# Padding that gives all matmul operands one offset within 512 bytes, and a write of normed rows split over two steps of the experts

## The chip, the cores and the metric

One core of a Trainium2 chip runs one program. The metric is the device time of one execution in microseconds (us), taken several times. Matmuls run on TensorE (PE; its weight loads are PEld), elementwise work on VectorE (DVE) and ScalarE (ACT), and GpSimd (POOL) issues a few of the transfers (DMA). The queue of SyncE (SP) issues the weight transfers.

## The reference

Two layers of a generator over 256 latent rows and 256 context rows of 1024 numbers. The first layer has a spatial-gating branch and an attention branch, then a dense SwiGLU of width 2816 (the FFN). The second has a gated recurrence, then a mixture of eight SwiGLU experts (the MoE), each of width 2816, of which every latent row uses two:

```python
def swiglu(t, w1, w3, w2):
    return (jax.nn.silu(t @ w1) * (t @ w3)) @ w2

logits = (t @ router_w).astype(jnp.float32)
top_v, top_i = lax.top_k(logits, TOP_K)
gk = jax.nn.softmax(top_v, axis=-1)
for e in range(N_EXPERTS):
    out = out + gates[:, e:e + 1] * swiglu(t, w1[e], w3[e], w2[e])
```

Everything is float32.

## The kernel before, in words

**Products.** A float32 product is made from three products of rounded halves (`mm3`, lines 358 to 361): both operands are cut into a high and a low part of type float32r, and PE runs high times high (line 359), high times low (360) and low times high (361). Weights come from DRAM in units of 1 MB (or 768 KB) into "raw" tiles; ACT casts half a unit to its high part `wh` (line 126) and DVE subtracts to get the low part `wl` (line 127). Raw tiles form a ring and `wh`/`wl` tiles another; a transfer waits on SP until the raw tile that it fills was cut by ACT and DVE.

**Places in SBUF.** Tiles are laid out pool after pool, each tile rounded up to 32 bytes per partition. Pools that open later begin where the ones below them end, so a small tile's size moves everything behind it. Modulo 512 bytes, summed up from the tile sizes, the start addresses of the float32r operands before are:

| operand | where | start modulo 512 before | after |
|---|---|---|---|
| `wh`, `wl` (cut weights) | all stages | 128 | 128 |
| `hH`, `hL` (cut activations), `hLa`, `hLb` | all stages | 128 | 128 |
| `mg` (cut hidden rows of an expert) | MoE, second product | 128 | 128 |
| `gH`, `gL` (cut hidden rows of the FFN) | FFN, second product | 192 | 128 |
| `xTH` (high part of an expert's input) | MoE, first products | 64 | 128 |
| `KH`, `KL` and half of the queries (`QS`) | attention | 448, 192, 192 | 128 |
| `disp` (dispatch matrix of the first two experts) | MoE, start | 64 | 128 |

The slices that the products read start at multiples of 512 bytes inside these tiles. The raw tiles of the pool `rawB` begin at 256 before and at 320 after.

**The MoE.** An expert's width is cut into three groups g of 1024, 1024 and 768. A step k is one expert e and one group g; there are 24. In step k, `moe_p` (line 1462) makes the first two products (`m1`, `m3`; the moving operand is the weight, the stationary one the expert's input `xTH`/`hLa`), `moe_t` turns the result into `mg`, and `moe_o` (line 1509) makes the second product of step k-1 with `mg` as the stationary operand. Experts 0 and 1 get their inputs by a matmul with a dispatch matrix. The others get theirs by a table: the normed rows are written to DRAM (`Hd`), the row numbers of each expert's places are scattered to DRAM (`Td`, four transfers in `places`, line 1559) and read back (`slots_of`), and `rows_of` (line 1434) gathers the rows of two experts from `Hd` with indirect transfers. `turn_slots` (line 1441) transposes and modulates them at e odd, g = 2, for the next two experts.

**What sets the order there.** The loop over k (line 1665) emits the work; a scheduler orders it, and `tc.issue_after(x)` keeps what it covers behind instruction x on its engine. All of this case's work at k = 1 stands behind the last cut of weights emitted by then:

```python
if k == 1:
    with tc.issue_after(st.last[0].ins), tc.issue_after(st.last[1].ins):
        route_rest()
        places()
        norm_rows()
```

`norm_rows` (line 1613) makes the normed rows in four pieces of 128x512 on ACT, each into a tile `ht` of a ring of two (line 595), and POOL issues the write of each piece to `Hd`. So the third piece needs the first write to have landed, and the fourth the second. `route_rest` (line 1358) is small work of DVE with one exponential on ACT, for which ACT loads a table. The gather of experts e+2 and e+3 is emitted at e even, g = 2 (line 1675).

Of the kernel before, what the change touches and what calls it, by code (L numbers as in the profile page):

```python
# [12 lines left out]
F32 = mybir.dt.float32  # L13
# [3 lines left out]
AF = mybir.ActivationFunctionType  # L17
# [4 lines left out]
P = 128  # L22
# [7 lines left out]
NE = 8  # L30
# [198 lines left out]
@contextmanager  # L229
def aligned(pool):  # L230
    with pool as p:
        yield Aligned(p)
# [3 lines left out]
def tile_block(ctx, tc, a, out):  # L236
    nc = tc.nc
    V, S, T = nc.vector, nc.scalar, nc.tensor
# [82 lines left out]
    for k in range(len(steps) + 1):  # L321
        if k < len(steps):
            e, g = steps[k]
            units += moe_p_units(e, g, m1[e], m3[e])
        if k > 0:
            e, g = steps[k - 1]
# [12 lines left out]
    def nm(s):  # L339
        ctr[0] += 1  # L340
        return f"{s}_{ctr[0]}"
# [7 lines left out]
    def tr():  # L349
        return bank("tr", 2)  # L350

    def po():
        return bank("po", 2)
# [46 lines left out]
    st = Stream(nc, units, slots, hslots, "")  # L400
# [4 lines left out]
    Xl = cp.tile([P, 2, D], F32, name="Xl")  # L405
# [13 lines left out]
    def big(tag, shape, dt):  # L419
        return lp.tile(shape, dt, tag=tag, name=nm(tag))  # L420

    esA = ctx.enter_context(ExitStack())
    cpA = esA.enter_context(tc.tile_pool(name="constA", bufs=1))
    gates["ao", 2, 0] = cpA.tile([P, D], F32, name="gate_o2")
    VT = cpA.tile([P, 3, P], F32, name="VT")
    sp8, nsp8 = [cpA.tile([P, 20], F32, name=f"lam{i}") for i in range(2)]
    esG = esA.enter_context(ExitStack())
    gpE = esG.enter_context(tc.tile_pool(name="gateE", bufs=1))
    Xc = gpE.tile([P, 2, D], F32, name="Xc")
    act = gpE.tile([P, KT, 32], F32, name="act")  # L430
    rw = gpE.tile([P, KT, NE], F32, name="rw")
    selb = gpE.tile([P, 2 * P + 8], F32, name="selb")[:, 0:2 * P]

    def small_e(shape, tag, **kw):
        return gpE.tile(shape, F32, tag=tag, name=nm(tag), **kw)
# [158 lines left out]
    def ht():  # L594
        return lp.tile([P, 512], F32, tag="ht", bufs=2, name=nm("ht"))
# [101 lines left out]
    with ExitStack():  # L697
# [22 lines left out]
        p = tr()  # L720
# [3 lines left out]
        p = tr()  # L724
# [41 lines left out]
        def ada_step(n, pump=True):  # L766

            s = ada_mm("ae", n, pump)
            if pend:
                ada_fin(*pend.pop())  # L770
            pend.append(("ae", n, s))


        with aligned(tc.tile_pool(name="e1", bufs=1)) as sp:
# [67 lines left out]
            for u in range(2):  # L842
# [1 line left out]
                    S.activation(uT[:, 2 * u + j, :], p, AF.Gelu_apprx_tanh)  # L844
                ws_pair(("u", u), hH, hL, ev)
                ada_step(5 + u)
            mv = sp.tile([P, 16, 2], F32, name="mv")
            for t in range(NT):
                for g in range(4):
                    bs = small_e([P, 6], "bs", bufs=2)  # L850
# [31 lines left out]
            p = tr()  # L882
# [4 lines left out]
            p = tr()  # L887
# [3 lines left out]
            for g in range(4):  # L891
                p = po()
# [14 lines left out]
            for u in range(4):  # L907
                wH, wL = views(st.get(("q", u // 2)), 2)
                for c in range(4):
                    cs = slice(P * c, P * c + P)  # L910
# [171 lines left out]
        with aligned(tc.tile_pool(name="ffn", bufs=1)) as sp:  # L1082
# [61 lines left out]
            for t in range(NT):  # L1144
                for h in range(2):
                    tk, cs = slice(P * t, P * t + P), slice(512 * h, 512 * h + 512)
                    p = po()
# [12 lines left out]
        with aligned(tc.tile_pool(name="odd", bufs=1)) as sp:  # L1160
# [112 lines left out]
            for b in range(NB // 2):  # L1273
# [19 lines left out]
                if b < NB // 2 - 1:  # L1293
                    for k in range(2):
                        wH, wL = st.get(("woo", b), pump=k == 0)
                        for t in range(2):
                            for h in range(2):
                                tk, cs = slice(P * t, P * t + P), slice(512 * h, 512 * h + 512)
# [9 lines left out]
            for t in range(2):  # L1308
                for h in range(2):
                    tk, cs = slice(P * t, P * t + P), slice(512 * h, 512 * h + 512)  # L1310
# [5 lines left out]
            rr, sqs = {}, {}  # L1316
            for t in range(2):
                sqs[t] = sq = small.tile([P, 2], F32, tag="sq", name=nm("sq"))
                for h in range(2):
                    cs, tk = slice(512 * h, 512 * h + 512), slice(P * t, P * t + P)  # L1320
                    last_v = resid("ao", 2, t, h, accs[t, h])
                    p = (tr, mm)[t]()
# [11 lines left out]
        moe = ctx.enter_context(aligned(tc.tile_pool(name="moe", bufs=1)))  # L1334
# [23 lines left out]
        def route_rest():  # L1358

            d = moe.tile([P, 4, 2], F32, name="dr")  # L1360
            g12.append(d)
            V.tensor_tensor(d[:, 0], mx[:, :, 1], mx[:, :, 0], op=ALU.subtract)
            S.activation(d[:, 1], d[:, 0], AF.Exp)
            V.tensor_scalar(d[:, 2], d[:, 1], 1.0, None, op0=ALU.add)
            V.reciprocal(d[:, 2], d[:, 2])
            V.tensor_tensor(d[:, 3], d[:, 1], d[:, 2], op=ALU.mult)
            for i in range(2):
                V.tensor_scalar(G[:, i, :], M1[:, i, :], d[:, 2, i:i + 1], None, op0=ALU.mult)
                V.scalar_tensor_tensor(G[:, i, :], M2[:, i, :], d[:, 3, i:i + 1], G[:, i, :],
                                       op0=ALU.mult, op1=ALU.add)  # L1370
            p = po()
            for i in range(2):
                T.matmul(p[:, 0:NE], one, M[:, i, :], start=(i == 0), stop=(i == 1))
            V.tensor_copy(cnt_p, p[:, 0:NE])
            ov, rk, hit, jk = [moe.tile([P, NE], F32, name=k) for k in ("ov", "rk", "hit", "jk")]
            V.tensor_scalar(ov, cnt_p, float(P), None, op0=ALU.is_gt)
            V.memset(rk, 0.0)
            for e in range(1, NE):
                V.tensor_tensor(rk[:, e:e + 1], rk[:, e - 1:e], ov[:, e - 1:e], op=ALU.add)
            cnt = moe.tile([P, 8], F32, name="cnt")  # L1380
            V.memset(cnt, 0.0)
            for j in range(3):
                V.scalar_tensor_tensor(hit, rk, float(j), ov, op0=ALU.is_equal, op1=ALU.mult,
                                       accum_out=cnt[:, j:j + 1])
                V.scalar_tensor_tensor(jk, hit, 1.0, e8, op0=ALU.mult, op1=ALU.mult, accum_out=cnt[:, 4 + j:5 + j])
                for i in range(2):
                    for c, src in enumerate((pos, M, G)):
                        V.scalar_tensor_tensor(jk, hit, 1.0, src[:, i, :], op0=ALU.mult, op1=ALU.mult,
                                               accum_out=ovf[:, j, i, c:c + 1])
            V.tensor_copy(ovi, cnt)  # L1390
# [3 lines left out]
        Hd = dram.tile([2 * P, D], F32, name="Hd")  # L1394
        Yd = dram.tile([(NE - 1) * P + 1, D], F32, name="Yd")
# [38 lines left out]
        def rows_of(idx):  # L1434

            r = big("hH", [P, len(idx), D], F32)
            for x, ids in enumerate(idx):
                nc.gpsimd.indirect_dma_start(r[:, x, :], None, Hd[:, :], bass.IndirectOffsetOnAxis(ap=ids, axis=0))
            return r
# [157 lines left out]
        zero = moe.tile([P, 8], I32, name="zero")  # L1597
        put, take = [moe.tile([P, 2, 2], I32, name=k) for k in ("put", "take")]
        slots_of = moe.tile([P, NE], I32, name="slots")
        tokf, toki = moe.tile([P, 2], F32, name="tokf"), moe.tile([P, 2], I32, name="toki")  # L1600
        lts = moe.tile([P, 1], F32, name="lts")
        g12, table = [], []

        def tokens():
# [5 lines left out]
                V.tensor_scalar(tokf[:, i:i + 1], lts, -1.0, float(P * i + P - 1), op0=ALU.mult, op1=ALU.add)  # L1610
            V.tensor_copy(toki, tokf)

        def norm_rows():

            nc.gpsimd.dma_start(Yd[(NE - 1) * P:, :].rearrange("o (p f) -> (o p) f", p=P), zero.bitcast(F32))
            for t in range(2):
                for h in range(2):
                    cs = slice(512 * h, 512 * h + 512)
                    r = ht()
                    S.activation(r, Xl[:, t, cs], AF.Copy, scale=rr[t])  # L1620
                    nc.gpsimd.dma_start(Hd[P * t:P * t + P, cs], r)

        d0 = moe.tile([P, 2, 256], F32R, tag="disp", name="disp0")
        dsp[0] = d0
# [1 line left out]
        for t in range(2):  # L1626
# [15 lines left out]
            p = tr()  # L1642
# [22 lines left out]
        for k in range(len(steps) + 2):  # L1665
            if k < len(steps):
                e, g = steps[k]
                s1 = moe_p(st, e, g, xT[e], P * (e % 2))
                st.behind = None
                if e == NE - 1 and g == 1:  # L1670
                    d = dsp[NE // 2 - 1]
                    dTs[e] = turn_disp(lambda i: d[:, i, P:2 * P])
                if e == NE - 2 and g == 1:
                    make_disp(NE // 2 - 1)
                if e % 2 == 0 and g == 2 and e + 2 < NE:
                    table[:] = [rows_of([slots_of[:, x:x + 1] for x in (e + 2, e + 3)])]
                if e % 2 == 1 and g == NG - 1 and e + 1 < NE:
                    turn_slots((e + 1, e + 2), table.pop())
            if k >= 2 and steps[k - 2] == (NE - 1, NG - 1):
                combine(NE - 1, dTs.pop(NE - 1), lambda i: G[:, i, NE - 1:NE])  # L1680
            last_step = k == len(steps) - 1
            if k == 0 or last_step:
                st.run_todo(tc, True)
            if last_step:
                st.later(4, lambda: moe_t(st, steps[-1], g, s1, True))
            if k == 1:
                with tc.issue_after(st.last[0].ins), tc.issue_after(st.last[1].ins):
                    route_rest()
                    places()
                    norm_rows()  # L1690
            if 1 <= k <= len(steps):
                last_t = moe_o(st, *steps[k - 1], steps[k - 1])
                if steps[k - 1][1] == NG - 1:
                    moe_y(steps[k - 1][0])
                if steps[k - 1] == (NE - 2, NG - 1):
                    table[:] = [combine_table()]
                if steps[k - 1] == (NE - 1, 0):
                    with tc.issue_after(st.last[1].ins):
                        add_table(table.pop())
            if k < len(steps) - 1:  # L1700
                with tc.issue_after(last_t.ins):
                    moe_t(st, steps[k], g, s1)
# [88 lines left out]
```

## Time and profile before

| | |
|---|---|
| median of three runs | 1596.05 us (1596.04 to 1596.6) |
| the profiled execution | 1594.75 us |
| its span | 1592.9 us |
| mean granted clock of TensorE | 0.991 of full speed |
| PE busy | 1537.1 us (96%), 7400 matmuls |
| weight loads (PEld) busy | 1221.9 us (77%) |
| DVE busy | 1271.2 us (80%) |
| ACT busy | 980.7 us (62%) |
| POOL busy | 34.1 us (2%) |
| read from DRAM | 401.01 MB |

The profiled execution is 1.3 us below the median of the three runs. The 1.85 us between it and its span lie before the first and after the last instruction. The ends of matmuls in the profile are modelled, so the length of one matmul says little; the distance between the starts of two neighbours is what PE spent on the first.

### The profile page before, as it was taken

Reading aid. Unit: us, or ns where it says so; the run is one execution under the profiler, and the core shown is the slowest. Engines: PE = TensorE matmul, PEld = TensorE weight load, DVE = VectorE, ACT = ScalarE, POOL = GpSimd, SP = SyncE. Lnnn points to the kernel's source line nnn. Section 1 sums busy time; section 2 is a strip of 40 time slices with the busy share of each in tenths; the row PEclk is TensorE's granted clock in tenths of the full one; section 3 lists DMA queues with packets and bytes.
Section 4 is the critical chain, followed back from the end, with each engine's and each line's share of the span. In section 5 each row is a group of like instructions: output and inputs, shape, how many; then the busy total and the mean of one; then the engine's idle time right before and its main releaser. Section 6 shows DMA issues by size and latency. Waiting matters only on the chain. (4 is left out here: it accounts for less than half of the span.)

```text
span 1592.9 us, 20155 instructions
## 1 busy us (share of the span) xinstructions
PE 1537.1 (96%) x7400; PEld 1221.9 (77%) x7400; DVE 1271.2 (80%) x1819; ACT 980.7 (62%) x1307; POOL 34.1 (2%) x33
## 2 busy tenths in 40 slices
PE   5999999999999999999998999999999999999996
PEld 3775787888888887776577888888878888788885
DVE  3577557475868586599998998999989999899997
ACT  4435625322222224679677878878788877877775
POOL 0000000000000000000001200000000000000010
PEclk9999999999999999999999999999999999999998
DMA  8867143434536431414697999999999999999991
GB/s 296 288 219 236 48 140 107 158 132 159 185 132 212 158 133 45 154 54 157 214 308 241 378 414 403 410 343 415 340 382 375 364 409 336 360 360 377 399 364 42
DMA packets 158362, 408.18 MB, mean 256 GB/s; under 512 B 8746, under 2 KB 50984, under 8 KB 158256
## 3 DMA queue, kind: packets, MB, share of 16 engines
q1 hardware_dynamic: 152288, 395.34, 68.9%
q0 software_dynamic: 2992, 9.98, 1.6%
q10 hardware_dynamic: 2976, 1.50, 0.4%
q8 instruction: 60, 0.98, 0.3%
q14 instruction: 46, 0.38, 0.1%
HBM read 401.01 MB, written 5.78 MB: 255 GB/s over the span
## 5 line engine op out<-in xcount | busy, mean ns | idle before, releaser
L126 ACT CAST wh<-raw 128x1024 fp32r<-128x1024 f32 (+2 forms) x676 | 671.5, 1006 | 454.1 <-PE mm L360 145.0
L127 DVE TENSOR_TENSOR wl<-raw,wh 128x1024 fp32r<-128x1024 f32 (+2 forms) x676 | 765.4, 1164 | 143.6 <-ACT wh L126 131.4
L361 PE MATMUL mm<-wh,hLa 128*128 128x512 f32 (+1 forms) x800 | 298.3, 374 | 0.0
L360 PE MATMUL mm<-wl,xTH 128*128 128x512 f32 (+1 forms) x768 | 287.6, 375 | 1.1 <-DVE wl L127 1.1
L359 PE MATMUL mm<-wh,xTH 128*128 128x512 f32 (+1 forms) x768 | 269.0, 377 | 1.7 <-DVE xTH L1406 1.0
L359 PE MATMUL mm<-hH,wh 128*128 128x512 f32 (+1 forms) x608 | 228.7, 378 | 1.7 <-ACT gT L1171 1.5
L361 PE MATMUL mm<-hH,wl 128*128 128x512 f32 (+1 forms) x608 | 224.7, 371 | 0.5 <-DVE wl L127 0.5
L361 PEld LDWEIGHTS mm<-wh,hLa 128*128 128x128 f32 x800 | 150.5, 188 | 28.5
L360 PEld LDWEIGHTS mm<-wl,xTH 128*128 128x128 f32 x768 | 144.6, 188 | 28.3 <-DVE wl L127 1.8
L359 PEld LDWEIGHTS mm<-wh,xTH 128*128 128x128 f32 x768 | 143.5, 188 | 27.5 <-DVE xTH L1406 1.2
L360 PE MATMUL po<-wl,mg 128*128 128x512 f32 x340 | 134.1, 395 | 2.3 <-DVE wl L127 2.3
L361 PE MATMUL po<-wh,mg 128*128 128x512 f32 x340 | 133.6, 393 | 0.0
L359 PEld LDWEIGHTS mm<-hH,wh 128*128 128x128 f32 x608 | 114.2, 189 | 24.1 <-issue 2.0
L361 PEld LDWEIGHTS mm<-hH,wl 128*128 128x128 f32 x608 | 114.4, 188 | 20.2 <-DVE wl L127 0.7
L359 PE MATMUL po<-wh,mg 128*128 128x512 f32 x340 | 115.9, 396 | 6.0 <-ACT wh L126 6.0
L360 PE MATMUL mm<-hLb,wh 128*128 128x512 f32 (+1 forms) x304 | 112.9, 372 | 0.6 <-DVE hLb L639 0.6
L360 PE MATMUL mm<-hLa,wh 128*128 128x512 f32 (+1 forms) x304 | 112.8, 371 | 0.5 <-DVE hLa L639 0.5
L523 DVE SCALAR_TENSOR_TENSOR xn<-raw,act,xn 128x512 f32<-128x512 f32 x112 | 81.7, 747 | 1.0
L359 PEld LDWEIGHTS po<-wh,mg 128*128 128x128 f32 x340 | 63.9, 189 | 20.3 <-ACT wh L126 7.3
L360 PEld LDWEIGHTS po<-wl,mg 128*128 128x128 f32 x340 | 64.1, 189 | 18.5 <-DVE wl L127 5.4
L361 PEld LDWEIGHTS po<-wh,mg 128*128 128x128 f32 x340 | 64.2, 189 | 13.1
L360 PE MATMUL po<-wl,gH 128*128 128x512 f32 x176 | 69.8, 397 | 0.0
(420 smaller groups left out, 1842.1 us busy)
## 6 DMA issues: line engine op xcount, KB each, us to landing
raw<-in_moe_w_dram SPq DMA_DIRECT2D x216, 1024.0 KB
raw<-in_moe_w_dram SPq DMA_DIRECT2D x64, 768.0 KB
raw<-in_ffn_w_dram SPq DMA_DIRECT2D x33, 1024.0 KB
raw<-in_ada_w_e_dram SPq DMA_DIRECT2D x24, 1024.0 KB
raw<-in_ada_w_o_dram SPq DMA_DIRECT2D x24, 1024.0 KB
raw<-in_w_in_o_dram SPq DMA_DIRECT2D x10, 1024.0 KB
raw<-in_w_in_e_dram SPq DMA_DIRECT2D x7, 1024.0 KB
raw<-in_w_out_o_dram SPq DMA_DIRECT2D x5, 1024.0 KB
```

The costliest lines, as they stand in the source:

```text
L126: sp = (self.nc.scalar.copy(hv, src), self.nc.vector.tensor_tensor(lv, src, hv.bitcast(F32), op=ALU.subtract))
L127: self.nc.vector.tensor_tensor(lv, src, hv.bitcast(F32), op=ALU.subtract))
L359: T.matmul(dst, aH, bH, start=start, stop=False)
L360: T.matmul(dst, aH, bL, start=False, stop=False)
L361: return T.matmul(dst, aL, bH, start=False, stop=stop)
L523: V.scalar_tensor_tensor(acc[s_], w[:, k, :], c, acc[s_], op0=ALU.mult, op1=ALU.add)
```

## The change

Four small tiles get longer, so that the tiles behind them move; `norm_rows` takes one half of the rows (t = 0 or 1) per call, the first half at k = 1 ahead of `route_rest` and `places`, the second at k = 2; the gather is emitted at e odd, g = 0 for experts e+1 and e+2, one step later than before.

```diff
-    sp8, nsp8 = [cpA.tile([P, 20], F32, name=f"lam{i}") for i in range(2)]
+    sp8, nsp8 = [cpA.tile([P, 64], F32, name=f"lam{i}")[:, :20] for i in range(2)]
...
-    selb = gpE.tile([P, 2 * P + 8], F32, name="selb")[:, 0:2 * P]
+    selb = gpE.tile([P, 2 * P + 40], F32, name="selb")[:, 0:2 * P]
...
-            mv = sp.tile([P, 16, 2], F32, name="mv")
+            mv = sp.tile([P, 96], F32, name="mv")[:, :32].rearrange("p (a b) -> p a b", a=16)
...
-        lts = moe.tile([P, 1], F32, name="lts")
+        lts = moe.tile([P, 32], F32, name="lts")[:, :1]
...
-        def norm_rows():
-
-            nc.gpsimd.dma_start(Yd[(NE - 1) * P:, :].rearrange("o (p f) -> (o p) f", p=P), zero.bitcast(F32))
-            for t in range(2):
-                for h in range(2):
-                    cs = slice(512 * h, 512 * h + 512)
-                    r = ht()
-                    S.activation(r, Xl[:, t, cs], AF.Copy, scale=rr[t])
-                    nc.gpsimd.dma_start(Hd[P * t:P * t + P, cs], r)
+        def norm_rows(t):
+
+            if t == 0:
+                nc.gpsimd.dma_start(Yd[(NE - 1) * P:, :].rearrange("o (p f) -> (o p) f", p=P), zero.bitcast(F32))
+            for h in range(2):
+                cs = slice(512 * h, 512 * h + 512)
+                r = ht()
+                S.activation(r, Xl[:, t, cs], AF.Copy, scale=rr[t])
+                nc.gpsimd.dma_start(Hd[P * t:P * t + P, cs], r)
...
-                if e % 2 == 0 and g == 2 and e + 2 < NE:
-                    table[:] = [rows_of([slots_of[:, x:x + 1] for x in (e + 2, e + 3)])]
+                if e % 2 == 1 and g == 0 and e + 1 < NE:
+                    table[:] = [rows_of([slots_of[:, x:x + 1] for x in (e + 1, e + 2)])]
...
             if k == 1:
                 with tc.issue_after(st.last[0].ins), tc.issue_after(st.last[1].ins):
+                    norm_rows(0)
                     route_rest()
                     places()
-                    norm_rows()
+            if k == 2:
+                with tc.issue_after(st.last[0].ins):
+                    norm_rows(1)
```

The paddings by their sizes: the two `lam` tiles grow from 96 to 256 bytes each (together 320), `selb` by 128, `mv` by 256, `lts` by 64. The FFN's and the attention's pools therefore move by 448 bytes (192 to 128 modulo 512), what stands behind `mv` by 704 (448 to 128), and the MoE's tiles behind `lts` by 64.

## Rows read from the trace of the kernel before

**Rows 1.** Busy time by stretch: window, PE, PEld, DVE, ACT, POOL, clock, DMA share, GB/s.
```profile
865.00:870.00 5.00, 2.75 (x6) 1.87 (x7) 3.24 (x10) 4.92 (x6) 2.47 (x2) 0.50 0.32 74
900.00:1000.00 100.00, 99.98 (x484) 83.49 (x484) 92.69 (x93) 82.49 (x98) 10.35 (x5) 1.00 1.02 410
```
**Rows 2.** Timeline of PE, FFN second product, operands at 128 and 192: start, length, what.
```profile
404.62 0.39 PE L359 MATMUL po<-wh,gH 128*128 128x512 f32 x1
...
412.79 0.39 PE L361 MATMUL po<-wh,gL 128*128 128x512 f32 x1
```
**Rows 3.** Timeline of PE, MoE second product, both operands at 128.
```profile
1144.08 0.63 PE L359 MATMUL po<-wh,mg 128*128 128x512 f32 x2
...
1154.76 0.40 PE L361 MATMUL po<-wh,mg 128*128 128x512 f32 x1
```
**Rows 4.** Timeline of PE, MoE first products of expert 1 and expert 3, operands at 128 and 64.
```profile
902.76 0.40 PE L360 MATMUL mm<-wl,xTH 128*128 128x512 f32 x1
...
924.31 0.40 PE L361 MATMUL mm<-wh,hLa 128*128 128x512 f32 x1
...
1122.16 0.39 PE L360 MATMUL mm<-wl,xTH 128*128 128x512 f32 x1
...
1143.86 0.39 PE L361 MATMUL mm<-wh,hLa 128*128 128x512 f32 x1
```
**Rows 5.** Groups by line and form: count, busy us, mean ns, idle before.
```profile
L360 PE MATMUL mm<-wl,xTH 128*128 128x512 f32 x640 | 252.0, 394 | 1.1 <-DVE wl L127 1.1
L360 PE MATMUL po<-wl,gH 128*128 128x512 f32 x176 | 69.8, 397 | 0.0
```
**Rows 6.** Timeline of PE: a 768-wide first product (512 and 256 columns); 256 columns alone, all at 128.
```profile
1254.15 0.40 PE L360 MATMUL mm<-wl,xTH 128*128 128x512 f32 x1
...
1270.40 0.28 PE L361 MATMUL mm<-wh,hLa 128*128 128x256 f32 x1
...
744.08 0.28 PE L360 MATMUL mm<-hLa,wh 128*128 128x256 f32 x1
...
749.58 0.28 PE L361 MATMUL mm<-hH,wl 128*128 128x256 f32 x1
```
**Rows 7.** Timeline of PE in the attention's scores, 512 columns.
```profile
139.62 0.40 PE L952 MATMUL mm<-KH_swT,QS 128*128 128x512 f32 x1
139.94 0.50 PE L955 MATMUL mm<-KL,xn 64*128 64x512 f32 x1
```
**Rows 8.** Timeline of PE around the stop at 862 us: in brackets idle time, releaser.
```profile
862.00 0.39 PE L361 MATMUL po<-wh,mg 128*128 128x512 f32 x1
866.78 0.80 PE L359 MATMUL po<-wh,mg 128*128 128x512 f32 x1 [4.39 <-ACT wh L126]
...
871.20 0.51 PE L359 MATMUL mm<-wh,xTH 128*128 128x512 f32 x2
```
**Rows 9.** Timeline of ACT, the normed rows.
```profile
855.06 1.34 ACT L1620 ACTIVATE ht<-Xl,n1r 128x512 f32<-128x512 f32 x2
...
865.08 0.72 ACT L1620 ACTIVATE ht<-Xl,n1r 128x512 f32<-128x512 f32 x1 [5.32 <-DMA Hd<-ht]
```
**Rows 10.** Groups of DVE from 850 to 900 us.
```profile
L127 DVE TENSOR_TENSOR wl<-raw,wh 128x1024 fp32r<-128x1024 f32 x18 | 21.5, 1221 | 6.0 <-ACT wh L126 5.3
```
**Rows 11.** Timeline of POOL: writes of rows, read of the slots, gathers.
```profile
856.08 1.15 POOL L1621 DMA_DIRECT2D Hd<-ht  x2 [58.68 <-ACT ht L1620]
...
890.07 0.95 POOL L1580 DMA_DIRECT2D slots<-Td  x1 [5.51 <-DMA Td<-toki,put]
897.83 7.97 POOL L1438 DMA_INDIRECT hH<-Hd,slots  x1 [6.82 <-DMA slots<-Td]
...
988.68 1.88 POOL L1438 DMA_INDIRECT hH<-Hd,slots  x1 [52.67 <-PE tr L1449]
```
**Rows 12.** Timeline of ACT: the first use of gathered rows.
```profile
985.09 1.47 ACT L1404 ACTIVATE ht<-tr,AB 128x256 f32<-128x256 f32 x3
```
**Rows 13.** Transfers that write or read the slots, gathers among them: issue to landing.
```profile
DMA to landing us min/median/max: 6.2/8.7/14.5
```
**Rows 14.** Waits of the SP queue from 780 us on: total us, times, longest.
```profile
SPq L112 <- DVE wl L127: 591.7, 254, 8.3
```

## The prediction

> **What bounds the kernel now.** I read the busy times by stretch first. In the middle of the MoE (900 to 1000 us [rows 1]) PE is busy all the time at full granted clock, DVE for 93%, and the transfers move 410 GB/s. Two engines and the transfers are thus near their limits, so the next question is who waits for whom. The waits of SP's queue [rows 14] answer it: of the 813 us from 780 us to the end, 592 are spent waiting for DVE to give a raw tile back. Transfers are paced by the work, and the work by PE. In the FFN it is PE too. So the time is the sum of what PE spends per matmul, plus the places where it stops, and the change touches both.
>
> The length of a matmul in the profile is modelled. I therefore take runs of matmuls that follow each other without a wait, and divide the time from the first start to the last by the number of steps between. That gives, for 512 columns: 36 matmuls of the FFN's second product, (412.79 - 404.62)/35 = 233.4 ns [rows 2]; 48 of the MoE's second product, 10.68/47 = 227.2 ns [rows 3]; 95 of its first products, 21.55/94 = 229.3 ns and 21.70/94 = 230.9 ns [rows 4]. These are the same operation, with the same moving tiles `wh`/`wl` at 128 modulo 512. What differs is where the stationary operand lies: 192 in the slow case, 128 in the fast one, 64 for two of three matmuls in the middle one. The correlation is what the change is about; that the offset is the cause no row shows, since the stages differ as well.
>
> The stops come from the timeline. The largest one in the MoE is at 862 us [rows 8]: nine matmuls take from 862.00 to 871.20, 9.20 us where 9 x 0.227 = 2.04 would do, so 7.2 us are lost. Of these PE is idle for 4.39 before the first of them, and afterwards runs at granted clock 0.50, the 1.2 GHz level, for some 5 us (865 to 870 [rows 1]). The reason named is ACT, which owed a cut of weights. ACT itself stood for 5.32 us in front of the fourth normed piece, waiting for the second write to `Hd` to land [rows 9], because the ring `ht` has two tiles.
>
> **The change, part by part.**
>
> *The split of the normed rows.* After it the calls at k = 1 take two tiles of a ring of two, whose last users are long done; neither waits. The 5.32 us wait has no successor there, and ACT returns to the cuts about 6 us earlier, at about 859 us, before PE runs dry at 862. That removes up to 7.2 us. But DVE also has the small instructions of `route_rest` and `places` in that place, and the cuts cost it 1.22 us [rows 10] where PE takes 6 x 0.227 = 1.36 us for half a unit: 0.14 us of slack each. Today ACT's stop hides part of the small work. Uncovered, it may cost PE nothing, or the rest of the small work that lies ahead of and between the next cuts, about 2 us at most. I take 1.0, because PE's 4.39 us stop began only 3 us after the last cut was ready. So the stop gives 6.2 us (5.2 to 7.2).
>
> The two pieces moved to k = 2 are 1.34 us of ACT together [rows 9], in front of cuts. The same 1.34 us stand at 855 us today, with a table load and one more piece behind them, and PE ran on until 862; I take nothing (at worst 1.3 us). Their ring tiles were written out 20 us before. Their writes queue on POOL behind the four scatters and the read of the slots at 890.07 [rows 11]; the pieces wait in tiles that nobody wants until the turn at 985.09 [rows 12]. The first gather, now at 897.83, comes behind these two writes. A write there takes POOL 1.15 us per two, and its landing some microseconds; nothing is queued behind the gather until the first expert's result. With the largest landing of 14.5 us [rows 13] the rows are there before 925 us, 60 us ahead of the turn. The two later gathers wait for the turn before theirs to free their tile (988.68 [rows 11]), 180 us ahead of need; being emitted a step later costs them nothing.
>
> *The offsets.* FFN, second product: 3 x 176 matmuls [rows 5], 233.4 to 227.2: 528 x 6.2 = 3.3 us. MoE, first products of the groups of 1024: 16 runs of 96 = 1536 matmuls, from the mean of the two runs, 230.1, to 227.2: 1536 x 2.9 = 4.5 us. The group of 768 alternates three matmuls of 512 and three of 256 columns, 172.9 ns on average [rows 6]. If its 512s take 230.1, its 256s take 115.6. The only run of 256 columns with all operands at 128 takes 5.50/46 = 119.6 ns [rows 6], slower. By that row the group would go to (227.2 + 119.6)/2 = 173.4; with the 256s left alone to 171.4. Over 768 matmuls that is +0.4 or -1.2 us; I take the measured row, +0.4. The attention's scores take 0.32 us for 512 columns [rows 7], 0.09 over the fast value; with 32 such matmuls 3 us could be there. But matmuls over half the rows and float32 transposes stand around them, the products with `xTH` lose only 0.003 for a similar mismatch, and I take nothing. Float32 matmuls, `disp` and the raw tiles' places: nothing; the transfers into the raw tiles have slack as long as SP waits for DVE. Sum of the offsets: 3.3 + 4.5 - 0.4 = 7.4 us (0 to 12).
>
> *Sum.* 6.2 + 7.4 = 13.6 us. The profiled execution, 1594.75, would become 1581.15; the median lies 1.3 above it, so I forecast 1596.05 - 13.6 = 1582.4.
>
> **The rivals.**
>
> *The offset is not the cause (B).* The differences of 2 to 6 ns between stages might come from the output bank, the rate of transfers or the order of the stationary operands. For it: the first products differ among themselves (229.3 against 230.9) at equal offsets. Against it: within the MoE, a few us apart and under the same traffic, runs alternate between 231 and 227 with the stationary tile, and the FFN at a quarter of the traffic has the slowest. Time: 1596.05 - 6.2 = 1589.9. The Trainium skill, "TensorE: Matmul & The Clock Gate", Part 2, states the rule behind this rival: moving operand and weight load have read ports of their own, and loading the next weights takes no read bandwidth from the running matmul. By that rule the offsets give nothing; what the trace can say is that it does not show why equal matmuls differ by 6 ns.
>
> *The stop moves (C).* ACT leaves the wait, but DVE's small work and the cuts then collide, or the second half at k = 2 finds its ring tile still in a write. For it: DVE is at 93%. Against: 20 us lie between. All 7.2 lost again in another place gives 1596.05 - 7.4 = 1588.7.
>
> *Slower: a gather that comes too late (D).* Its code now stands behind the second half of the rows and one step later; if POOL's order puts it behind waits that end after the turn, ACT stands at the first modulation, and behind it every cut. It decides when a gather is issued later than 985.09 - 14.5 = 970 us for the first pair, 73 us after today. Price: up to 14.5 us [rows 13] for each of the three pairs, 43.5 together, 1582.4 + 43.5 = 1625.9; one pair alone would be hidden in the gain. The distance of 73 us speaks against it.
>
> *Neither part acts (E).* The scheduler puts both halves side by side again, and the offset is inert: 1596.
>
> **How the numbers follow.** Forecast (A) 0.62, B 0.12, C 0.12, D 0.07, E 0.07. A measurement of this kernel can tell about 0.2%, 3.2 us, from no change. A, B and C lie more than that below 1596.05: faster 0.86. E is the same, 0.07; D slower, 0.07. A's own range takes the bounds: 1582.4 - 1.0 (all of the stop) - 1.6 (the 256s left alone) - 3.0 (scores) = 1576.8 below, and above 1582.4 + 1.0 + 1.3 and half of the MoE's 4.5, 1587. To take in B and C the range goes to 1590.5; A, B and C hold 0.86, and their edges leave about 0.8.
>
> **What would show it.** Runs of the FFN's second product at 227 ns instead of 233.4, and of the MoE's first products at 227 to 228: the offsets. If they stand where they were, B. The 768 group at 173.4 or 171.4 tells of the 256s. No idle time over 1 us of PE between 855 and 890 us, no wait of ACT for `Hd`, full clock there: the split. A wait of ACT's first modulation at the turn for a gather would be D. The prediction is wrong if the spacing goes up anywhere, or if PE's idle time in the MoE after 890 us grows by more than 2 us.

## The result, and the profile after

| | before | after |
|---|---|---|
| median, of four runs each | 1596.05 us (1593.2 to 1596.6) | 1582.16 us (1581.57 to 1585.44) |
| the profiled execution, its span | 1594.75, 1592.9 us | 1581.62, 1579.9 us |
| PE busy | 1537.1 us | 1529.1 us |
| mean granted clock | 0.991 | 0.992 |

The ratio of after to before is 0.9921, with a 95% interval of 0.9903 to 0.9939: 13.9 us by the medians, 13.0 by the two spans. The forecast was 1582.4.

The first two lines of the page for the kernel after. DVE and ACT are as busy as before; PE is busy for 8.0 us less with the same 7400 matmuls, and the other 5 us of the span are time in which it used to stand.

```profile
span 1579.9 us, 20155 instructions
...
PE 1529.1 (97%) x7400; PEld 1219.9 (77%) x7400; DVE 1270.7 (80%) x1819; ACT 980.9 (62%) x1307; POOL 29.6 (2%) x33
```

The timeline of PE after, in the order of time: the first and last matmul of the FFN's second product that use `gH`, a run in its middle as in [rows 2] with the matmul ahead of it, the place of the stop [rows 8], the two runs of [rows 4], the run of [rows 3] and the 768 group of [rows 6].

```profile
300.11 0.39 PE L359 MATMUL po<-wh,gH 128*128 128x512 f32 x1
...
404.59 0.47 PE L359 MATMUL po<-wh,gH 128*128 128x512 f32 x1
404.89 0.40 PE L360 MATMUL po<-wl,gH 128*128 128x512 f32 x1
...
412.62 0.39 PE L361 MATMUL po<-wh,gL 128*128 128x512 f32 x1
...
628.44 0.39 PE L360 MATMUL po<-wl,gH 128*128 128x512 f32 x1
...
859.50 0.39 PE L361 MATMUL po<-wh,mg 128*128 128x512 f32 x1
859.73 0.39 PE L359 MATMUL po<-wh,mg 128*128 128x512 f32 x1
...
893.59 0.39 PE L360 MATMUL mm<-wl,xTH 128*128 128x512 f32 x1
...
914.91 0.39 PE L361 MATMUL mm<-wh,hLa 128*128 128x512 f32 x1
...
1111.96 0.39 PE L360 MATMUL mm<-wl,xTH 128*128 128x512 f32 x1
...
1133.31 0.39 PE L361 MATMUL mm<-wh,hLa 128*128 128x512 f32 x1
1133.54 0.61 PE L359 MATMUL po<-wh,mg 128*128 128x512 f32 x2
...
1144.19 0.40 PE L361 MATMUL po<-wh,mg 128*128 128x512 f32 x1
...
1243.02 0.39 PE L360 MATMUL mm<-wl,xTH 128*128 128x512 f32 x1
...
1259.47 0.28 PE L361 MATMUL mm<-wh,hLa 128*128 128x256 f32 x1
```

Distances between the starts say what PE spends per matmul. Second product of the FFN, 35 matmuls: (412.62 - 404.89)/34 = 227.4 ns, where it was 233.4. This leaves out the step of the run's first matmul, which now takes 0.30 us (404.59 to 404.89) and took 0.23 before; with it the 36 take 8.03/35 = 229.4. First products of the MoE, 95 each: 21.32/94 = 226.8 and 21.35/94 = 227.1, where they were 229.3 and 230.9. Second product of the MoE, 48: 10.65/47 = 226.6, where it was 227.2. These three now take nearly the same, at equal offsets. One stage got slower: the group of 768, 95 matmuls, takes 16.45/94 = 175.0 ns on average, where it was 172.9.

The stop is gone. The matmul that started at 862.00 before [rows 8] starts at 859.50 now, and the next, which came 4.78 us later, follows 0.23 us behind. The windows say the same of the engines. Columns as in [rows 1]:

```profile
860.00:865.00 5.00, 5.00 (x27) 3.80 (x25) 5.00 (x18) 3.10 (x4) 1.11 (x1) 1.00 0.77 63
865.00:870.00 5.00, 5.00 (x30) 4.34 (x29) 5.00 (x16) 3.92 (x7) 0.61 (x1) 1.00 1.02 414
...
900.00:1000.00 100.00, 99.96 (x483) 83.65 (x482) 93.20 (x93) 83.20 (x99) 6.68 (x5) 1.00 1.03 408
```

PE is busy throughout at clock 1.00, the 2.4 GHz level, where it had been busy for 2.75 of 5 us at 0.50, the 1.2 GHz level. DVE is full too, 5.00 of 5, but PE has no idle time between 855 and 890 us. From 900 to 1000 us PE, DVE, ACT and the transfers are as busy as before [rows 1].

The timelines of ACT and of POOL after, the rows that answer to [rows 9, 11, 12]:

```profile
852.62 1.33 ACT L1620 ACTIVATE ht<-Xl,n1r 128x512 f32<-128x512 f32 x2
...
882.49 1.34 ACT L1620 ACTIVATE ht<-Xl,n1r 128x512 f32<-128x512 f32 x2
...
975.70 1.47 ACT L1404 ACTIVATE ht<-tr,AB 128x256 f32<-128x256 f32 x3
...
890.01 1.12 POOL L1621 DMA_DIRECT2D Hd<-ht  x2
...
899.47 1.85 POOL L1438 DMA_INDIRECT hH<-Hd,slots  x1 [8.34 <-PE mm L361]
```

Both pairs of normed pieces run on ACT without a wait. The later pair's writes are issued at 890.01, and the first gather at 899.47, 1.6 us later than before. The wait of the gather that ends last is for PE (8.34 us), not for the writes. The first modulation at 975.70 waits for nothing: 76 us lie between.

### The profile page after: what moved, and what is told of

Its sections match the earlier page's. It is cut to its first block, busy times and chain, and to the rows that moved or that the text cites. A ratio compares the mean times of both kernels' runs of the same rounds, so it can differ in the third digit from the quotient of the medians.

```text
span 1579.9 us, 20155 instructions
## 1 busy us (share of the span) xinstructions
PE 1529.1 (97%) x7400; PEld 1219.9 (77%) x7400; DVE 1270.7 (80%) x1819; ACT 980.9 (62%) x1307; POOL 29.6 (2%) x33
## 4 chain that ended last, share of the span: by engine, by line
PE 84%; DVE 8%; ACT 3%; DMA 2%; issue 1%; ACTq 0%; DVEq 0%
PE mm L360 18%; PE mm L359 18%; PE mm L361 18%; PE po L360 7%; PE po L361 7%; PE po L359 7%; DVE wl L127 1%; PE po L453 1%; PE tr L1496 1%; ACT wh L126 1%; PE po L1006 1%; PE tr L991 1%; DVE xn L523 1%; DMA raw<-in_ada_w_o_dram 1%; DMA raw<-in_w_in_e_dram 1%
## 5 line engine op out<-in xcount | busy, mean ns | idle before, releaser
L359 PEld LDWEIGHTS mm<-hH,wh 128*128 128x128 f32 x608 | 114.1, 188 | 24.0 <-issue 2.0
L359 PE MATMUL po<-wh,gH 128*128 128x512 f32 x176 | 69.2, 393 | 0.0
```

The costliest lines, as they stand in the source:

```text
L359: T.matmul(dst, aH, bH, start=start, stop=False)
```

## The experiments

Times are medians, and ratios are to runs of the kernel before on the same chip. Its median was 1595.04 us beside experiments 1 to 4, and 1596.46 beside 5 to 8. A kernel that ran once has a time without an interval; its spacings say more.

### 1. The split alone

The kernel before with the new `norm_rows(t)`, its two calls and the later gather, without the paddings:

```diff
...
             if k == 1:
...
+                    norm_rows(0)
                     route_rest()
                     places()
-                    norm_rows()
+            if k == 2:
+                with tc.issue_after(st.last[0].ins):
+                    norm_rows(1)
```

> The split of the normed rows and the later gather, without the four paddings. Theory (two independent parts): the stop of PE at 862 us is gone, the spacing of matmuls stays as before (FFN second product 233.4 ns, MoE first products 229.3 to 230.9, the group of 768 172.9); 7 us less than before, about 1589, range 1587 to 1591. Rival C (the stop only moves to another place): 1595 to 1596 with a new idle stretch of PE of several us between 855 and 900 us. Rival: the parts need each other (the split pays only at the faster spacing): under 3 us.

Measured: 1588.29 us, ratio 0.9953 [0.9938, 0.9969], against 1595.04 for before: 6.8 us. PE's timeline of this run, for [rows 2] and the second run of [rows 4]:

```profile
405.06 0.39 PE L359 MATMUL po<-wh,gH 128*128 128x512 f32 x1
...
413.23 0.39 PE L361 MATMUL po<-wh,gL 128*128 128x512 f32 x1
...
1114.36 0.39 PE L360 MATMUL mm<-wl,xTH 128*128 128x512 f32 x1
...
1136.05 0.39 PE L361 MATMUL mm<-wh,hLa 128*128 128x512 f32 x1
```

and its windows:

```profile
860.00:865.00 5.00, 5.00 (x22) 3.75 (x21) 5.00 (x16) 3.79 (x5) 0.58 (x2) 1.00 0.76 125
```

The spacings stand where they were: 8.17/35 = 233.4 ns and 21.69/94 = 230.7. The stop is gone, and it does not come back elsewhere: PE has no idle time from 855 to 890 us, and 5.1 us after that, as before. Rival C would have left about nothing, and the run gives 6.8 (by the interval, 4.9 to 9.9). The rival that the split pays only at the faster spacing falls too.

### 2. The paddings alone

The kernel before with the four longer tiles and nothing else:

```diff
-    sp8, nsp8 = [cpA.tile([P, 20], F32, name=f"lam{i}") for i in range(2)]
+    sp8, nsp8 = [cpA.tile([P, 64], F32, name=f"lam{i}")[:, :20] for i in range(2)]
...
-        lts = moe.tile([P, 1], F32, name="lts")
+        lts = moe.tile([P, 32], F32, name="lts")[:, :1]
```

> The four paddings alone; normed rows and gather as before. Theory: the FFN's second product and the MoE's first products go to 227 ns, the group of 768 to 175, the stop at 862 us stays (ACT waits some 5 us for the write of rows); 6 to 7 us less than before, about 1589.5. Rival B (the spacing comes from something else that the whole change altered, for example the missing stop or the order): spacing 229 to 233 as before, 1596.

Measured: 1587.73 us (1585.42 to 1590.97), ratio 0.9948 [0.9933, 0.9963], 7.3 us below 1595.04 (by the interval, 5.9 to 10.7). PE's timeline, the profiled execution being the longest of the six:

```profile
405.27 0.40 PE L360 MATMUL po<-wl,gH 128*128 128x512 f32 x1
...
413.00 0.39 PE L361 MATMUL po<-wh,gL 128*128 128x512 f32 x1
...
859.90 0.39 PE L361 MATMUL po<-wh,mg 128*128 128x512 f32 x1
865.61 0.79 PE L359 MATMUL po<-wh,mg 128*128 128x512 f32 x1 [5.32 <-ACT wh L126]
...
1121.29 0.39 PE L360 MATMUL mm<-wl,xTH 128*128 128x512 f32 x1
...
1142.64 0.39 PE L361 MATMUL mm<-wh,hLa 128*128 128x512 f32 x1
```

ACT's timeline and the windows, in two fences:

```profile
863.90 0.72 ACT L1620 ACTIVATE ht<-Xl,n1r 128x512 f32<-128x512 f32 x1 [5.73 <-DMA Hd<-ht]
```

```profile
865.00:870.00 5.00, 3.92 (x8) 2.79 (x9) 4.41 (x13) 4.51 (x6) 2.39 (x2) 0.57 0.56 169
```

The spacings are those of after, 7.73/34 = 227.4 ns and 21.35/94 = 227.1, with the stop still in place, in this execution even longer: PE idle for 5.32 us behind ACT, which waits 5.73 for the write, and then a clock of 0.57. So the offsets alone make the matmuls shorter; rival B, by which this run would have had the time of before, falls. The two parts alone come to 6.8 + 7.3 = 14.1 us, the whole to 13.9: within what such medians can tell, they add up.

### 3. Another common offset

The kernel after, with 64 bytes ahead of all pools, so that every operand lies at 192 modulo 512:

```diff
-    LT = cp.tile([P, P], F32, name="LT")
+    LT = cp.tile([P, P + 16], F32, name="LT")[:, :P]
```

> The changed kernel with one more padding of 64 bytes ahead of all pools of weights and activations, so that all float32r operands start at 192 modulo 512 instead of 128. Theory (what counts is that the moving and the stationary operand have the same offset): 227 ns everywhere, 175 in the group of 768, time as the changed kernel, 1582. Rival (128 itself, a start at a multiple of 128 bytes, is what is fast): spacing 230 to 233 ns in all 512-column matmuls, some 5000 of them, so 15 to 30 us more, about 1605.

Measured: 1582.09 us, ratio 0.9910 [0.9892, 0.9928]. PE's timeline in the FFN's second product:

```profile
405.01 0.40 PE L360 MATMUL po<-wl,gH 128*128 128x512 f32 x1
...
412.74 0.39 PE L361 MATMUL po<-wh,gL 128*128 128x512 f32 x1
```

7.73/34 = 227.4 ns, and the first products that end at 1133.49 take 226.8; the group of 768 takes 175.1. Nothing differs from after: of the two places tried for all operands together, 128 and 192, neither is better, so it is the distance between the operands that counts.

### 4 to 6. Which distances cost

Three kernels that are the kernel after with two paddings changed; each ran once. Ahead of `gH`/`gL` the tile `facc` gets longer, and ahead of `xTH` the tile `lts`. The first of them, which puts `gH`/`gL` at 256 and `xTH` at 384:

```diff
-            acc = sp.tile([P, NT, D], F32, name="facc")
+            acc = sp.tile([P, NT * D + 32], F32, name="facc")[:, :NT * D].rearrange("p (t d) -> p t d", t=NT)
...
-        lts = moe.tile([P, 32], F32, name="lts")[:, :1]
+        lts = moe.tile([P, 96], F32, name="lts")[:, :1]
```

The others have 112 and 48 (`gH` at 64, `xTH` at 192), and 64 and 64 (`gH` at 384, `xTH` at 256), in place of 32 and 96. The pools of the FFN and the MoE round each tile up to 64 bytes, so `lts` has 64 bytes in the kernel before and 128 in the one after.

> The changed kernel with gH and gL moved to 256 modulo 512 (distance 128 from the weights) and xTH to 384 (distance 256); hLa stays at 128. Theory as the change words it (same offset within 512 bytes): any distance costs, 230 to 234 ns in the FFN's second product and 229 to 231 in the MoE's first products. Rival (a coarser rule, equality within 128 or 256 bytes is enough): 227 ns in both. The group of 768 tells whether its 256-column matmuls, slower since the change, get fast again (172 to 173) with any distance.

> The changed kernel with gH and gL at 64 modulo 512 (distance -64 from the weights) and xTH at 192 (distance +64); hLa stays at 128. Theory (equality within 256 bytes, from the run with distances 128 and 256): both distances cost, 231 to 234 ns in the FFN's second product and 229 to 231 in the MoE's first products, as +64 and -64 did before the change. Rival (only one sign costs, the stationary operand ahead of or behind the moving one): one of the two stays at 227.

> The changed kernel with gH and gL at 384 modulo 512 (distance 256) and xTH at 256 (distance 128): the two distances of the earlier run exchanged. Theory (period of 256 bytes): FFN second product 227, MoE first products about 230. Rival (period of 512, and the MoE's first products for some other reason fast at any distance but -64): FFN 230 to 234, MoE 227.

Measured: 1583.64, 1589.61 and 1588.28 us. PE's timeline of the first (`gH` at 256, `xTH` at 384):

```profile
405.72 0.40 PE L359 MATMUL po<-wh,gH 128*128 128x512 f32 x1
...
413.85 0.39 PE L361 MATMUL po<-wh,gL 128*128 128x512 f32 x1
...
1113.74 0.39 PE L360 MATMUL mm<-wl,xTH 128*128 128x512 f32 x1
...
1135.09 0.39 PE L361 MATMUL mm<-wh,hLa 128*128 128x512 f32 x1
```

of the second (`gH` at 64, `xTH` at 192):

```profile
404.36 0.39 PE L360 MATMUL po<-wl,gH 128*128 128x512 f32 x1
...
412.15 0.39 PE L361 MATMUL po<-wh,gL 128*128 128x512 f32 x1
...
1114.86 0.40 PE L360 MATMUL mm<-wl,xTH 128*128 128x512 f32 x1
...
1136.71 0.39 PE L361 MATMUL mm<-wh,hLa 128*128 128x512 f32 x1
```

and of the third (`gH` at 384, `xTH` at 256):

```profile
403.40 0.40 PE L360 MATMUL po<-wl,gH 128*128 128x512 f32 x1
...
411.13 0.39 PE L361 MATMUL po<-wh,gL 128*128 128x512 f32 x1
...
1113.38 0.40 PE L360 MATMUL mm<-wl,xTH 128*128 128x512 f32 x1
...
1135.25 0.39 PE L361 MATMUL mm<-wh,hLa 128*128 128x512 f32 x1
```

Divided as above (35 or 34 steps in the FFN, 94 in the MoE) and put beside the earlier runs, the spacing goes with the distance from the moving operand (at 128) to the stationary one:

| stationary minus moving, bytes | FFN second product, ns | MoE first products, ns |
|---|---|---|
| 0 | 227.4 (after) | 226.8, 227.1 (after) |
| +64 | 233.4 (before) | 21.85/94 = 232.4 (second) |
| +128 | 8.13/35 = 232.3 (first) | 21.87/94 = 232.7 (third) |
| +256 | 7.73/34 = 227.4 (third) | 21.35/94 = 227.1 (first) |
| -64 | 7.79/34 = 229.1 (second) | 229.3, 230.9 (before) |

In the MoE's column the distance holds for two of three matmuls; `hLa` stays at 0. The runs of 34 steps leave out a first step of 0.28 to 0.31 us, of the kind seen in the result. Over all 528 matmuls of the FFN's stage, from each start to the next, the order is the same: 229.7 ns at 0 and at +256, 231.3 at -64, 234.1 at +128, 234.6 at +64. Each distance is measured in both stages, while the MoE's second product, whose operands stay at 128, takes about 227 in all of these kernels; so neither the stage nor the traffic makes the difference. The paddings also move the tiles that lie behind in the same pool; moving all of them by 64 together (experiment 3) changed nothing. The expectation that any distance costs missed at 256: 256 bytes apart is as good as 0. So the padding need not make the offsets equal within 512; equal within 256 did as well. And the sign counts: in the FFN -64 costs about 2 ns and +64 costs 6. The second kernel's spacings therefore came out the other way round from what was expected, 229.1 in the FFN and 232.4 in the MoE: their size goes with the sign and not with the stage. The third's 232.7 in the MoE also lies above what was expected.

### 7 and 8. The group of 768

Here equal offsets had lost 2.1 ns per matmul. The runs above already bear on why. The same group of the same expert takes 172.8 ns with the split alone, 175.0 with the paddings alone, where the stop is still in place, and 174.9 to 175.1 in the kernels of experiments 3 to 6, with `xTH` at distance 0, 64, 128 or 256. So neither the missing stop nor the place of `xTH` made the group slower, and no distance tried there makes it fast again; only before, with `xTH` at -64 and `hLa` at 0, was it 172.9. In the kernel after, the cut weights of these groups alone are written 64 bytes (16 numbers) further into their tile, so that the distance there is -64 for all three matmuls:

```diff
...
-            return [(h[:, :n], l[:, :n], r[:, n * j:n * j + n])]
+            o = 16 if g == 2 else 0
+            return [(h[:, o:o + n], l[:, o:o + n], r[:, n * j:n * j + n])]
...
+                        ws = slice(cs.start + 16, cs.stop + 16) if g == 2 else cs
...
```

The second kernel has 48 in place of 16 (192 bytes, a distance of -192, which is +64 modulo 256).

> The changed kernel; in the groups of 768 the cut weights are written 64 bytes further into their tiles, so the stationary operands are at distance -64 there and at 0 elsewhere. Theory (what counts is the distance between the moving and the stationary start, and the best one depends on the pattern of 512 and 256 columns): the group of 768 goes from 175.0 back to about 172.8 ns as before the change, 768 matmuls, 1.7 us less than the changed kernel, about 1580.4. Rival (the place of xTH itself, or the missing stop, made that group slower): 175 stays.

> As the run before, with 192 bytes: distance -192, which is +64 modulo 256. Theory: not 175; if the sign does not matter 172 to 173, else up to 178. Rival (place of xTH or the missing stop): 175.

Measured: 1580.96 us, ratio 0.9899 [0.9882, 0.9915], for the first, and 1580.99 in one run for the second. PE's timeline of the first, three of its 768 groups (the added line moves 360 and 361 to 361 and 362):

```profile
1052.56 0.39 PE L361 MATMUL mm<-wl,xTH 128*128 128x512 f32 x1
...
1069.04 0.28 PE L362 MATMUL mm<-wh,hLa 128*128 128x256 f32 x1
...
1145.36 0.39 PE L361 MATMUL mm<-wl,xTH 128*128 128x512 f32 x1
...
1159.41 0.28 PE L362 MATMUL mm<-wh,hLa 128*128 128x256 f32 x1
```

The group at 1052 takes 16.48/94 = 175.3 ns, no better than after. The one at 1145 takes 14.05/82 = 171.3, 83 matmuls, and a third, from 1242.54 to 1258.68, 16.14/94 = 171.7. Of seven groups these two fell below the 172.8 that was expected; the other five take 174.8 to 175.6 (the eighth, in which PE waits, is left out). The groups at 1052 and 1242 are those of experts 2 and 4, and by the kernel's rings their operands lie at the same places in SBUF: one buffer of `xTH`, the same half of it, and 70 half units of cut weights per expert in a ring of 5. The same work at the same places thus runs in two ways. With +64 the seven groups take 173.4 to 174.0. The intervals of this kernel and of after overlap, so neither is shown to be better than after. From the starts of the same matmuls: before, the 512 columns of this pattern take 228.3 ns and the 256 columns 117.3; after, 231.9 and 118.0; in the good groups here 229.3 and 114.1, in the others 232.2 and 118.4. What lost is mainly the 512 columns next to the 256s. What decides between the two ways stays open.

## Why the prediction was right

**The stop.** It was put at 6.2 us (5.2 to 7.2). From the matmul at 862.00 [rows 8] to the one at 902.76 [rows 4] PE took 40.76 us, and now it takes 893.59 - 859.50 = 34.09: 6.7 us less. The split alone gave 6.8. The mechanism is the one that was named: ACT has no wait for `Hd`, PE none for ACT, and the clock stays at 1.00. The step that was too careful is the 1.0 us for DVE's uncovered small work. DVE is indeed full from 860 to 870 us, but that cost PE at most the half microsecond between 6.7 and 7.2, of which some 0.2 is the slower group of 768 that lies in this stretch. The pieces moved to k = 2 cost nothing that can be seen.

**The offsets.** The FFN was put at 3.3 us; from its first matmul with `gH` to its last, before took 331.11 us (299.20 to 630.31) and after takes 628.44 - 300.11 = 328.33: 2.8. Part of what is missing is a wait that the forecast did not have: faster matmuls come to some runs before DVE has read the output tile that they are to write. The weight load of the matmul at 404.59, in the timeline of after:

```profile
404.56 0.19 PEld L359 LDWEIGHTS po<-wh,gH 128*128 128x128 f32 x1 [0.23 <-DVE facc L1129]
```

and the waits from 299 to 632 us, before and then after (total us, times, longest):

```profile
PEld po L359 <- DVE facc L1129: 0.8, 2, 0.6
...
PEld po L359 <- DVE facc L1129: 1.8, 6, 0.7
```

The MoE's first products were put at 4.5: from 230.1 to 227.0 on 1536 matmuls it is 4.8. The step that was mis-sized is the group of 768. It was put at 0.4 us of loss, by the one run of 256 columns at 128; it lost (175.0 - 172.9) x 768 = 1.6. The forecast took the rate of each width from runs of that width alone, and the rates did not carry over to the mixed order: the 512s there went up, from 228.3 to 231.9 ns, where those of the 1024 groups went down, and the 256s stayed near 118 (the forecast had 230.1 to 227.2, and 115.6 to 119.6). Against it stands a gain that was not forecast, the second product of the MoE at 226.6 instead of 227.2 ns, some 0.6 us on 1020 matmuls if that run stands for all.

**The attention.** Nothing was taken, with up to 3 us possible: from the first of the scores' matmuls at line 952 to the last at line 955, 51.71 us before and 51.69 after. The cautious choice was right; the bound need not have been so wide. Where `KH` at 448 met the queries at 192, they were 256 bytes apart already, which by experiments 4 to 6 costs nothing.

**The sum.** 6.7 + 2.8 + 4.8 + 0.6 - 1.6 = 13.3, less 0.9 us by which this execution reached the FFN's second product later (300.11 against 299.20), is 12.4 against 13.0 by the spans. That start is no part of the change: over the kernels here it lies between 298.6 and 301.0, whatever the padding. The 1.6 counts all eight groups of 768, one of which is in the 6.7 already, so 0.2 of the missing 0.6 us is counted twice; the rest was not traced. The terms miss by up to 1.2 us each (the group of 768), some one way and some the other; that the total came within 0.3 us of the medians is luck in part.

**The signs.** The prediction was to be wrong if the spacing went up anywhere. It did, in the group of 768. The forecast itself had put that group up, from 172.9 to 173.4, so this sign did not fit it; what failed there is the size, as said above. The other sign did not appear: PE's idle time after 890 us is 5.1 us before and after.

**The rivals.** B falls by the paddings alone: the matmuls became shorter with the rest as before. The Trainium skill's "TensorE: Matmul & The Clock Gate", Part 2, gives the moving operand and the weight load read ports of their own and says that loading the next weights takes no read bandwidth from the running matmul. What the prediction drew from it for B, that the offsets give nothing, the runs do not bear out: the FFN's second product takes 227.4 ns at a distance of 256 bytes and 232.3 at 128. Why the distance counts no run here shows. C falls by the split alone. D was far off: the gather is issued at 899.47, where 970 was the point from which it would count. E falls with both.

## What to carry to other kernels

Where matmuls run back to back, each with a weight load of its own, compare runs of equal matmuls by the distance of their starts, stage by stage; a difference of a few ns can come from where the two operands lie, and a few padded bytes in a small tile try it (here: equal modulo 256 bytes was best for rows of 512 columns; and measure each pattern of widths, since mixed widths went the other way). A ring of two tiles that are emptied by transfers should not be asked for four in a row on an engine that others wait for: emit the work in two places, as far apart as its consumer allows.

## What was not expected of the hardware

- Two operands 256 bytes apart are as good as two at the same offset, 227 ns, while 64 and 128 bytes give some 232 to 233, and -64 some 229 to 231. Whether this repeats at larger distances was not tried.
- The same mixed run of 512 and 256 columns takes 171.3 or 175.3 ns per matmul in one execution of one kernel, with the operands at the same places.
- A stop costs more than its idle time: after 4.39 us without work the granted clock was 0.50, the 1.2 GHz level, from 865 to 870 us [rows 1, 8], and with the paddings alone, after 5.32 us, 0.57 from 865 to 870 and 0.75 from 870 to 875, between the 1.2 and the 2.4 GHz level.
